# A two-layer hybrid decoder on one core: TensorE's instruction order pinned in the mixing stage

## The chip, the cores and the metric

The kernel runs on one core of a Trainium2 chip. The core has TensorE for matmuls, VectorE (DVE in the rows), ScalarE (ACT) and GpSimd (POOL) for element-wise work, and DMA queues; the kernel's transfers are issued on SyncE's queue (SP). Each engine works through its own list of instructions in order and waits for semaphores that other engines or transfers raise. The metric is device time in microseconds; lower is better.

## The reference, cut to what matters

Two layers work on a sequence of 512 tokens of width 1024 in float32. Each layer is a SwiGLU feed-forward block, a mixing block and a second feed-forward block, each followed by a layer norm:

```python
for l in range(DEPTH):                                   # DEPTH = 2
    x = _layernorm(ALPHA * x + 0.5 * _swiglu(x, ffn1_w_in[l], ffn1_w_out[l]), ...)
    x = _layernorm(ALPHA * x + _hybrid_mixer(x, l, ...), ...)
    x = _layernorm(ALPHA * x + 0.5 * _swiglu(x, ffn2_w_in[l], ffn2_w_out[l]), ...)
```

The mixer makes one wide projection `h = x @ w_in`. Three causal mixers read parts of it: RWKV-7 (8 heads of 64), differential attention (4 heads) and a chunked gated DeltaNet (4 heads of 128). Each result goes through a branch matrix, is weighted by a sigmoid gate made from `h`, and the sum goes through `w_out`:

```python
branches = jnp.einsum('blnc,ncd->blnd', ys, w_branch)
gates = jax.nn.sigmoid(h[..., o3:].reshape(B, L, N_BRANCH, D_MODEL))
merged = jnp.einsum('blnd,blnd->bld', gates, branches)
return merged @ w_out
```

## The kernel before

All matrices are float32 and are multiplied as three products of rounded parts: each weight tile is split into `wh` (a cast on ScalarE) and `wl` (a subtraction on VectorE), and so is the transposed stream (`xTh`, `xTl`). One column of 128 outputs of a projection is thus 8 x 3 = 24 matmuls of 128x512 into one PSUM tile (`proj`, L440). The tiles are `pj` for the mixers, `pz` for DeltaNet's output gate, `pgt` for the merge's gates, `pg` and `pu` in the feed-forward stage.

The mixing stage (`mix`, L1378) is written by Python generators. `main` (L1327) first writes the two lora columns, then twelve units in the order R D R D R R D G G D G G, where R is a pair of RWKV heads, D a head of differential attention and G a DeltaNet head. A unit (`unit`, L1337) writes three projection columns (R and D) or four (G: three `pj`, one `pz`), 24 matmuls each, and then puts a head generator on the list `active`. The first unit is followed by 16 matmuls named `pab`. The first three columns of a stage (both lora columns and one of the first unit) are written ahead of it, under the name `pe`. After the units come three rounds of `merge` (L1290).

A head generator (`rw_pair`, `da_head`, `gdn_head`) yields between its steps. A step holds small matmuls and transposes on TensorE and element-wise work on the other engines. A planner, the class `Estimate`, keeps a clock for each engine from a formula for each instruction; when a step is written it notes in `stage` when the step's results should be there. Every projection yields after six matmuls, and `interleave` (L1372) then writes steps of active heads whose time has come, up to CAP = 1300 ns of TensorE's planned clock. A unit starts only when fewer than WIDTH = 4 heads are active:

```python
while sum(it[0] < 3 for it in self.active) >= WIDTH:
    self.pump(True)
```

Here `pump(True)` writes the next step of a head whose time has come or, when there is none, of the head that is due first. A head leaves the list with its last step. In all three kinds of head that step, or the end of it, is a group of four transposes named `pyT`, of the tile `Y` (R), `dO` (D) or `gO` (G).

In `rw_pair` the transposes `paT` (L933) give `R` on VectorE, and `pW` (L938) reads it in the same step. The step of `pb` splits `sq` first. `inverse` (L680) solves the triangular systems: rows on VectorE, a trip through DRAM, the transposes `iZ` on VectorE, and then matmuls named `ip`.

What is written this way isn't yet the order on an engine. The framework's scheduler walks a timing model of its own and lets an engine take a later instruction when an earlier one is not ready in that model. Only `load_x`, at the kernel's start, pins the order so far. A matmul of the mixing stage passes through `Queue.order` (L73), which adds the edge to the preceding instruction only where `inorder` is set.

Of the kernel before, what the change touches and what calls it, by code (L numbers as in the profile page):

```python
# [134 lines left out]
class Net:  # L135
# [1241 lines left out]

    def mix(self, l):  # L1378
        self.active, self.ys, self.yps, merged = [], [{}, {}, {}], {}, []
        self.interleave(self.main(merged))  # L1380
        acc = [[None, None] for _ in range(NT)]
        self.out_acc(merged[0:4], 0.5 / ALPHA, acc)
        self.out_last(merged[4:8], 0.5 / ALPHA, acc, self.a["ln2_g"][l], self.a["ln2_b"][l])
# [41 lines left out]
```

## Time and profile before

| | before |
|---|---|
| median of 3 runs | 2865.65 us (2860.83 to 2866.03) |
| the profiled execution, its time | 2866.84 us |
| its span, first to last instruction | 2865.0 us |
| mean granted TensorE clock | 0.995 of 2.4 GHz |
| mixing stage, first layer | 395.7 to 1018.7 us |
| mixing stage, second layer | 1817.4 to 2447.2 us |

The page's shares are averages over stages; the rows below go by stage and by instruction. All instructions carry the line L66, which is the helper that records them, so they are told apart by their tiles (`out<-in`). Where a row of the timeline ends in brackets, the engine was idle for so many us before it, until the named engine had written the named tile. Matmul durations are modelled and overlap: the distance from one start to the next tells more than the duration.

### The profile page before, as it was taken

The page shows a single profiled execution, that of the slowest core. Times are in us where ns is not written, and L with a number is a line of the kernel's source. Part 1 is how long each engine was busy: PE and PEld are TensorE (multiplying, and loading weights), DVE is VectorE, ACT ScalarE, POOL GpSimd, SP SyncE. Part 2 cuts the span into 40 slices and gives each one's busy share as a digit, 9 for nine tenths or more (in the row PEclk, how much of TensorE's full clock was granted, in tenths as well). Part 3 has the DMA queues.
Part 4 walks back from the last instruction along what each step waited for, and adds up shares of the span by engine and source line. Part 5 has one row for each costly group of instructions (what it writes and reads, how often), then busy time and mean ns, then how long its engine had stood idle before and what let it go on. Part 6 is the DMA issues. An engine that isn't in the chain of part 4 may idle for free. (4 is left out here: it accounts for less than half of the span.)

```text
span 2865.0 us, 40194 instructions
## 1 busy us (share of the span) xinstructions
PE 2817.8 (98%) x15728; PEld 2333.7 (81%) x15728; DVE 1657.9 (58%) x3760; ACT 1015.4 (35%) x1805; POOL 157.2 (5%) x205
## 2 busy tenths in 40 slices
PE   9999999999999999999999999999999999999998
PEld 8888887778878888888888888777788788888887
DVE  4333568788874463443643335677888745633345
ACT  3222345444543332222422223454445433322222
POOL 1000021010000010000100000210100000100001
PEclk9999999999999999999999999999999999999999
DMA  6433423222223353333533334222222234533332
GB/s 179 126 98 99 141 75 84 67 72 55 71 72 88 101 180 101 98 96 97 155 96 113 101 96 134 82 71 69 69 61 65 72 89 117 163 109 97 96 96 89
DMA packets 436350, 282.18 MB, mean 98 GB/s; under 512 B 39432, under 2 KB 391872, under 8 KB 436160
## 3 DMA queue, kind: packets, MB, share of 16 engines
q1 hardware_dynamic: 436160, 279.60, 33.5%
q8 instruction: 124, 2.03, 0.3%
q14 instruction: 66, 0.54, 0.1%
HBM read 258.31 MB, written 21.25 MB: 98 GB/s over the span
## 5 line engine op out<-in xcount | busy, mean ns | idle before, releaser
L66 DVE TENSOR_TENSOR wl<-wr,wh 128x1024 fp32r<-128x1024 f32 x406 | 500.1, 1232 | 655.7 <-ACT wh L66 652.4
L66 ACT CAST wh<-wr 128x1024 fp32r<-128x1024 f32 x406 | 427.4, 1053 | 1252.4 <-issue 550.9
L66 PE MATMUL pu<-xTh,wh 128*128 128x512 f32 x672 | 261.6, 389 | 0.0
L66 PE MATMUL pu<-xTh,wl 128*128 128x512 f32 x672 | 261.4, 389 | 0.0
L66 PE MATMUL pu<-xTl,wh 128*128 128x512 f32 x672 | 261.4, 389 | 0.0
L66 PE MATMUL oa<-wh,hl 128*128 128x512 f32 x640 | 249.0, 389 | 0.0
L66 PE MATMUL pg<-xTh,wh 128*128 128x512 f32 x640 | 249.0, 389 | 0.0
L66 PE MATMUL pg<-xTl,wh 128*128 128x512 f32 x640 | 249.0, 389 | 0.0
L66 PE MATMUL pg<-xTh,wl 128*128 128x512 f32 x640 | 249.0, 389 | 0.0
L66 PE MATMUL oa<-wh,hh 128*128 128x512 f32 x640 | 249.0, 389 | 0.0
L66 PE MATMUL oa<-wl,hh 128*128 128x512 f32 x640 | 249.0, 389 | 0.0
L66 PE MATMUL pj<-xTh,wh 128*128 128x512 f32 x560 | 229.1, 409 | 0.0
L66 PE MATMUL pj<-xTh,wl 128*128 128x512 f32 x560 | 227.7, 407 | 0.0
L66 PE MATMUL pj<-xTl,wh 128*128 128x512 f32 x560 | 225.7, 403 | 0.0
L66 DVE TENSOR_TENSOR ft<-ft,pu 128x512 f32<-128x512 f32 x84 | 57.7, 687 | 226.5 <-PE pu L66 226.4
L66 PE MATMUL pgt<-xTh,wh 128*128 128x512 f32 x384 | 153.0, 398 | 0.0
L66 PE MATMUL pgt<-xTh,wl 128*128 128x512 f32 x384 | 150.4, 392 | 0.0
L66 PE MATMUL pgt<-xTl,wh 128*128 128x512 f32 x384 | 150.3, 391 | 0.0
L66 PEld LDWEIGHTS pu<-xTh,wl 128*128 128x128 f32 x672 | 126.2, 188 | 26.2
L66 PEld LDWEIGHTS pu<-xTl,wh 128*128 128x128 f32 x672 | 126.2, 188 | 26.0
L66 PEld LDWEIGHTS pu<-xTh,wh 128*128 128x128 f32 x672 | 126.0, 188 | 26.2
L66 PEld LDWEIGHTS pg<-xTh,wh 128*128 128x128 f32 x640 | 120.2, 188 | 25.2
(397 smaller groups left out, 5295.5 us busy)
## 6 DMA issues: line engine op xcount, KB each, us to landing
wr<-in_ffn_w_in_dram SPq DMA_DIRECT2D x176, 512.0 KB
wr<-in_mix_w_in_dram SPq DMA_DIRECT2D x132, 512.0 KB
wr<-in_ffn_w_out_dram SPq DMA_DIRECT2D x88, 512.0 KB
wr<-in_mix_w_branch_dram SPq DMA_DIRECT2D x24, 512.0 KB
xres<-x SPq DMA_DIRECT2D x40, 256.0 KB
x<-xres SPq DMA_DIRECT2D x40, 256.0 KB
wr<-in_mix_w_out_dram SPq DMA_DIRECT2D x16, 512.0 KB
iX<-Xd SPq DMA_DIRECT2D x24, 256.0 KB
```

Of the source, the lines that this page charges most:

```text
L66: r = f(*args, **kw)
```

## The change

While the mixing stage is being written, TensorE's queue object is marked `inorder`. Each TensorE instruction of the stage then gets an edge to the TensorE instruction written just before it, so the scheduler has to keep them in written order. `last` is cleared first, so the stage's first instruction is tied to nothing. The other engines and the transfers are scheduled as before. No instruction is added or removed.

```diff
     def mix(self, l):
         self.active, self.ys, self.yps, merged = [], [{}, {}, {}], {}, []
+        queues = (self.est.tensor,)
+        for q in queues:
+            q.inorder, q.last = True, None
         self.interleave(self.main(merged))
+        for q in queues:
+            q.inorder = False
         acc = [[None, None] for _ in range(NT)]
```

## Rows read from the trace of the kernel before

**Rows 1.** The page: busy us of each engine (share of the span) xinstructions.
```profile
PE 2817.8 (98%) x15728; PEld 2333.7 (81%) x15728; DVE 1657.9 (58%) x3760; ACT 1015.4 (35%) x1805; POOL 157.2 (5%) x205
```
**Rows 2.** Stretches, the two mixing stages: busy us, TensorE clock, DMA share, GB/s.
```profile
395.70:1018.70 623.00, 608.88 (x4117) 495.82 (x4117) 455.38 (x1383) 281.39 (x608) 40.39 (x53) 1.00 0.29 77
1817.40:2447.20 629.80, 617.18 (x4118) 502.27 (x4117) 456.56 (x1382) 281.07 (x607) 39.20 (x52) 0.98 0.28 76
```
**Rows 3.** The page's costliest groups: busy us, mean ns; idle time and its releaser.
```profile
L66 DVE TENSOR_TENSOR wl<-wr,wh 128x1024 fp32r<-128x1024 f32 x406 | 500.1, 1232 | 655.7 <-ACT wh L66 652.4
...
L66 PE MATMUL pu<-xTh,wh 128*128 128x512 f32 x672 | 261.6, 389 | 0.0
...
L66 PE MATMUL pj<-xTh,wh 128*128 128x512 f32 x560 | 229.1, 409 | 0.0
```
**Rows 4.** Timeline of TensorE, projections alone: first and last of 30.
```profile
399.88 0.39 PE L66 MATMUL pj<-xTh,wh 128*128 128x512 f32 x1
...
406.45 0.39 PE L66 MATMUL pj<-xTh,wl 128*128 128x512 f32 x1
```
**Rows 5.** Timeline of TensorE around one projection matmul between small ones.
```profile
781.82 0.39 PE L66 MATMUL pgw<-iZ,rk 128*128 128x128 f32 x2
781.97 0.48 PE L66 MATMUL pj<-xTh,wl 128*128 128x512 f32 x1
782.28 0.38 PE L66 MATMUL pv<-rv,iZ 128*128 128x128 f32 x2
```
**Rows 6.** Stretches from a mixing stage's start: TensorE's matmuls into `pj` alone.
```profile
395.00:556.17 161.17, 97.04 (x379) 1.00 0.27 72
395.00:612.01 217.01, 130.64 (x506) 1.00 0.27 71
395.00:665.95 270.95, 153.54 (x585) 1.00 0.26 69
395.00:717.25 322.25, 187.51 (x715) 1.00 0.27 69
395.00:770.70 375.70, 214.32 (x815) 1.00 0.26 69
...
1817.00:2200.14 383.14, 219.46 (x815) 0.97 0.26 67
```
**Rows 7.** The same stretches, TensorE's matmuls into `pz` alone.
```profile
395.00:665.95 270.95, 5.60 (x24) 1.00 0.26 69
395.00:717.25 322.25, 12.06 (x48) 1.00 0.27 69
395.00:770.70 375.70, 17.94 (x72) 1.00 0.26 69
```
**Rows 8.** Timeline of all engines, the end of one R head.
```profile
716.41 0.69 DVE L66 TENSOR_TENSOR Y<-Y,gn 128x512 f32<-128x512 f32 x1
...
717.25 0.52 PE L66 MATMUL pyT<-ident,Y 128*128 128x128 f32 x3
```
**Rows 9.** Timeline of TensorE from `paT` to `pW` of one R unit.
```profile
498.42 0.60 PE L66 MATMUL paT<-ident,AR 128*128 128x128 f32 x4
498.78 0.48 PE L66 MATMUL pj<-xTh,wh 128*128 128x512 f32 x1
...
499.56 0.40 PE L66 MATMUL pj<-xTh,wh 128*128 128x512 f32 x1
500.83 0.43 PE L66 MATMUL pW<-iZ,R 128*64 128x128 f32 x3 [0.88 <-DVE R L66]
```
**Rows 10.** Timeline of TensorE: one head's `pyT` in the first and second layer.
```profile
556.17 0.52 PE L66 MATMUL pyT<-ident,Y 128*128 128x128 f32 x3 [1.94 <-DVE Y L66]
...
1982.45 0.52 PE L66 MATMUL pyT<-ident,Y 128*128 128x128 f32 x2 [2.52 <-DVE Y L66]
```
**Rows 11.** Stretches after that idle time in the second layer, columns as in Rows 2.
```profile
1982.00:1984.00 2.00, 1.55 (x6) 1.44 (x7) 1.87 (x9) 0.57 (x1) 0.00 (x0) 0.65 0.00 0
1984.00:1986.00 2.00, 2.00 (x9) 1.75 (x8) 0.70 (x2) 0.65 (x2) 0.00 (x0) 0.50 0.00 0
```

## The prediction

> **What bounds the kernel now.** I began with the page's line of engine shares: TensorE is busy for 98% of the span [rows 1], so this time goes down only if TensorE issues less or waits less, and it goes up by every wait that nothing fills. The reader should see there how little is left to win. Next came the stretches of the two mixing stages, the only ones that the change touches: 623.0 and 629.8 us, with TensorE busy for 608.9 and 617.2 of them [rows 2]. So 14.1 and 12.6 us are plainly idle. VectorE is busy for 455 us in either stage (73%), which makes it the engine that TensorE's small matmuls wait for. Last I read TensorE's own timeline, to see in which order its instructions run today, and compared that with the order in which the code writes them.
>
> The plain stream of projections runs at (406.45 - 399.88) / 29 = 0.2266 us from one matmul to the next [rows 4]. I use this step, and not the modelled durations of 389 and 409 ns [rows 3], as the price of one wide matmul. The heads' small matmuls are sprinkled into that stream.
>
> **What the change does to the order.** It adds no instruction and no byte. It ties each TensorE instruction of the stage to the one written before it. Today the scheduler lets a later instruction go first when, by its reckoning, the one in front has no data yet; the fillers are the wide projection matmuls. Afterwards TensorE stands still in those places.
>
> The largest of them can be counted. Before it writes the columns of a unit, `unit` drives the active heads until fewer than WIDTH = 4 are left. Each head's last TensorE step is its `pyT` group. So in the written order a `pyT` must come before the first projection of that unit. The units' columns are known (2 lora, 3 per R or D unit, 4 per G unit, 24 wide matmuls each, the first three columns done early). By the order in which heads start and in which their `pyT` groups run today, four heads are active at five unit starts: the fourth R unit and each of the four G units. At the third R, third D and fourth D units one of the four has already ended, so nothing is forced there.
>
> The fourth R unit may start after 14 columns, 336 wide matmuls. By the `pyT` at 556.17 us there have run 379 [rows 6]: 43 too early. The first G unit: 20 columns, 480; by 612.01 us 506 have run: 26. The second G unit: 24 columns, 576; by 665.95 us 585 `pj` and 24 `pz` have run [rows 6, 7]: 33. The third G unit: 31 columns, 744; by 717.25 us 715 + 48: 19. The fourth: 35 columns, 840; by 770.70 us 815 + 72: 47. Together 168 wide matmuls of each layer now run ahead of a step that is written before them; the second layer's last count is the same 815 [rows 6]. Priced at 0.2266 us they are 38.1 us per layer that today cover a wait.
>
> **How much of this cover turns into waiting.** Nothing, if data lies ready and TensorE only comes late to it; all of it, if the data comes no earlier. The nearest rows say mostly the second: at the third G unit, VectorE's last write of `Y` ends at 716.41 + 0.69 = 717.10 us, and `pyT` starts at 717.25, 0.15 us later [rows 8]. There TensorE is waiting for VectorE whatever it does meanwhile. And at 556.17 `pyT` idled 1.94 us even behind its five fillers [rows 10]. Against this: a filler overshoots the moment of readiness by half a matmul on average, and seven columns (168 / 24) fewer in these stretches means seven fewer weight splits of 1.23 us [rows 3] on VectorE in the middle of the chains that are waited for. I take two thirds: 25.4 us per layer, between bounds of one half (19) and all (38).
>
> **The small shifts elsewhere.** Some steps read, on TensorE, what VectorE or ScalarE makes within the same step: `pW` after `R`, `pb` after the split of `sq`, `ip` after the transposes of `iZ`. The row to look at: `paT` at 498.42, four projections, then `pW` at 500.83, idle 0.88 us for `R` [rows 9]. In written order these four come afterwards, so the wait grows by 4 x 0.2266 = 0.9 us. Per layer there are 4 R units with two such places and 8 inversions: 16 x 0.9 = 14.5 us, of which a good third lies inside the forced stretches already counted. I take 9 (estimate), bounds 3 and 16, since heads wait at the same time and one wait serves several.
>
> **What is won.** After a small group the next wide matmul takes 782.28 - 781.97 = 0.31 us instead of 0.2266 [rows 5], 0.08 us more. Some 38 such returns per layer vanish when the fillers leave the forced stretches (estimate, the 168 in gaps of four or five): 3 us.
>
> **The clock.** After the 2.52 us idle before `pyT` in the second layer [rows 10] the granted clock reads 0.65 and then 0.50, the lower level of 1.2 GHz, for the next two stretches of 2 us [rows 11]: (0.35 + 0.50) x 2 = 1.7 us lost. The first layer had 1.94 us idle at the same place [rows 10] and kept 1.00 throughout [rows 2]. The change makes some five waits of this length in each layer (one at the end of each forced stretch, estimate); if every second one is followed by such a spell, with the spell's loss partly inside other waits, that is 4 us per layer.
>
> The Trainium skill (TensorE: Matmul & The Clock Gate, section "HAM oscillation — how this bites in real kernels") says that a matmul kernel which waits between bursts drops to the low clock at each wait and pays for the warm-up again. By that rule all ten new waits would pay, 17 us in place of 8; the second layer's row agrees with it, the first layer's does not.
>
> **The sum.** Per layer 25.4 + 9 + 4 - 3 = 35.4 us, 70.8 for both. The profiled execution took 2866.84 us (span 2865.0 and 1.84 around it): 2937.6. It lies 1.2 us above the median of the three runs, so I say 2936 us. What is queued behind a waiting matmul are the next unit's projections, and behind these ScalarE's `sh` and `cv` passes and the weight casts; they only slide, as TensorE is the engine that all of them follow. Weight loads on SP's queue slide with them; DMA engines are busy for 0.29 [rows 2], so nothing collides. The merges after the last unit hold no small work at their end that could win anything back.
>
> **Rivals.** (1) *It pays, by fewer switches.* Mixing projections show up to 409 ns against 389 in the feed-forward stage [rows 3]: 20 ns x 1680 `pj` is 34 us at most that the sprinkling costs, and 26.7 us are idle [rows 2]. If a fixed order halved both and the forced waits were filled, about 30 us would go: 2836. It decides where fewer than 15 / 0.2266 = 66 of the 168 fillers of a layer become waits. The late `Y` speaks against it; the idle rows, which show that the scheduler's guess is often wrong, for it. Chance 0.08.
> (2) *Only the single shifts cost.* While a chain is late, other heads' small work that today runs behind `pyT` may be written ahead of it and fill the gap. Then 9 + 2 - 3 = 8 us per layer: 2881. Against it: the scheduler would have run such work in place of a projection, had it been ready. Chance 0.13.
> (3) *It costs more.* One late small matmul also holds back small ones of other heads, which today slip past as well, and all waits come with the low clock: 38 + 16 + 9 = 63 us per layer, 2992 and beyond. The trace shows such slipping only in passing. Chance 0.12.
> (4) *The order was nearly there*, no difference: the counts speak against it. Chance 0.04.
>
> **How the numbers follow.** The forecast has 0.63. Its own bounds are 19 + 3 - 4 = 18 and 38 + 16 + 8 = 62 us per layer, 2901 to 2990. The range from 2876 to 2995 takes in rival 2 and the lower edge of rival 3. A difference under 0.2% can't be told from none here. Faster 0.08, within 0.2% 0.05, slower 0.87.
>
> **What would show it.** In the profile after, each of the five counts should read exactly 336, 480, 576, 744 and 840 before its `pyT`, with idle rows "<-DVE Y", "<-DVE iZ", "<-DVE dsc" on TensorE; TensorE's idle time should grow by 60 us or more over the two stages, and the feed-forward stages stay as they are. Returns from small to wide should be fewer. The prediction is wrong if the counts are met and yet TensorE idles no more than today (the data was ready), or if the stage's clock falls well under 0.95 (the spells weigh more than I take).

## The result and the profile after

The pinned kernel takes 3019.41 us (median of 4 runs, 3012.95 to 3020.03) against 2865.84 us (4 runs, 2860.83 to 2870.67): ratio 1.0531, 95% interval 1.0508 to 1.0554. It is slower, as forecast, but by 154 us where I had 71, and above the range. The profiled execution took 3020.03 us, its span is 3018.3 us and its mean granted clock 0.973.

The page's line of engine shares, to be read against [rows 1]:

```profile
PE 2860.4 (95%) x15728; PEld 2376.4 (79%) x15728; DVE 1666.7 (55%) x3760; ACT 1018.6 (34%) x1805; POOL 153.6 (5%) x205
```

The same instructions ran. TensorE's busy time grew by 43 us and its share still fell from 98% to 95%. The stretches of the two mixing stages, columns as in [rows 2]:

```profile
396.04:1098.19 702.15, 633.89 (x4116) 520.04 (x4114) 460.43 (x1383) 282.75 (x607) 38.15 (x53) 0.95 0.26 69
1896.94:2599.91 702.97, 634.65 (x4116) 520.62 (x4115) 460.13 (x1382) 282.64 (x606) 37.85 (x52) 0.95 0.25 68
```

Against [rows 2] they grew by 79.2 and 73.2 us, 152 of the 153 us by which the span grew: the feed-forward stages did not move. TensorE is plainly idle for 68.3 us in each (702.15 - 633.89 and 702.97 - 634.65), where it was idle for 14.1 and 12.6: 54.1 + 55.7 = 109.8 us more. The clock reads 0.95 where it read 1.00 and 0.98. VectorE's busy time is within 6 us of before.

The counts of projections before the five `pyT` groups that close a head before a unit may start, columns as in [rows 6], with the busy times of the other engines that touch the tile behind TensorE's; first those into `pj`:

```profile
395.00:578.75 183.75, 88.41 (x336) 64.69 (x336) 11.44 (x16) 13.61 (x22) 0.91 0.23 60
395.00:638.49 243.49, 126.07 (x480) 90.48 (x480) 16.43 (x23) 19.14 (x31) 0.92 0.24 61
395.00:704.32 309.32, 144.31 (x552) 103.48 (x552) 23.11 (x32) 21.75 (x35) 0.92 0.23 59
395.00:768.40 373.40, 182.37 (x696) 130.69 (x696) 32.54 (x45) 27.88 (x45) 0.93 0.23 60
395.00:829.37 434.37, 200.93 (x768) 144.17 (x768) 39.17 (x54) 29.91 (x48) 0.93 0.23 58
```

and those into `pz`, as in [rows 7]:

```profile
395.00:704.32 309.32, 7.61 (x24) 5.16 (x24) 0.69 (x1) 0.58 (x1) 0.92 0.23 59
395.00:768.40 373.40, 13.61 (x48) 9.52 (x48) 1.37 (x2) 1.17 (x2) 0.93 0.23 60
395.00:829.37 434.37, 19.49 (x72) 13.95 (x72) 2.05 (x3) 1.74 (x3) 0.93 0.23 58
```

336, 480, 552 + 24 = 576, 696 + 48 = 744, 768 + 72 = 840: the five forecast numbers to the last matmul. From the end of the last projection to the `pyT` that ends each forced stretch TensorE then did this (length, TensorE's busy time, clock, DMA share, GB/s):

```profile
541.84:578.75 36.91, 27.87 (x361) 0.86 0.13 32
637.32:638.49 1.17, 1.17 (x34) 1.00 0.00 0
683.54:704.32 20.78, 17.77 (x312) 1.00 0.11 28
763.78:768.40 4.62, 1.29 (x9) 1.00 0.23 55
804.05:829.37 25.32, 17.68 (x139) 0.82 0.13 33
```

The idle time in them is 9.0 + 0 + 3.0 + 3.3 + 7.6 = 23.0 us (23.3 in the second layer). I had forecast 25.4. The other 68.3 - 23.0 = 45.3 us of the stage's idle time stand at other places, where I had added 9. Here are the longest of the profile's waits of TensorE over the whole program, those in the forced stretches included (total us, times, longest):

```profile
PE pG L66 <- DVE gg L66: 14.7, 2, 7.4
PE pk L66 <- DVE gL L66: 14.1, 16, 1.9
PE pyT L66 <- DVE gO L66: 12.2, 6, 2.8
PE pb L66 <- ACT sqh L66: 11.9, 4, 3.3
PE pW L66 <- DVE R L66: 11.2, 8, 3.1
PE ppT L66 <- DVE dsc L66: 11.1, 8, 3.5
PE pkk L66 <- ACT AR L66: 9.6, 8, 1.4
```

The longest of all, `pG`, lies far from any forced stretch, in the DeltaNet scalars near the stage's start. Here is TensorE's timeline around it, after:

```profile
421.24 0.39 PE L66 MATMUL pj<-xTh,wl 128*128 128x512 f32 x1
428.98 0.61 PE L66 MATMUL pG<-gg,m_le 128*128 128x16 f32 x2 [7.36 <-DVE gg L66]
```

and before:

```profile
427.55 0.39 PE L66 MATMUL pj<-xTl,wh 128*128 128x512 f32 x1
429.91 0.40 PE L66 MATMUL pG<-gg,m_le 128*128 128x16 f32 x2 [1.97 <-DVE gg L66]
```

The data for `pG` came at about the same moment in both. What differs is how many projections had run by then. The stretch up to `pG`, `pj` alone, before:

```profile
395.00:429.91 34.91, 26.36 (x113) 21.15 (x113) 3.55 (x5) 4.62 (x8) 1.00 0.24 64
```

and after:

```profile
395.00:428.98 33.98, 18.50 (x78) 14.50 (x78) 2.87 (x4) 2.53 (x4) 0.93 0.23 62
```

113 against 78: the scheduler had let 35 projections slip past `pG`, almost six whole groups of six, at a place for which I had allowed nothing.

### The profile page after: what moved, and what is told of

Its sections match the earlier page's. It is cut to its first block, busy times and chain, and to the rows that moved or that the text cites. A ratio compares the mean times of both kernels' runs of the same rounds, so it can differ in the third digit from the quotient of the medians.

```text
span 3018.3 us, 40200 instructions
## 1 busy us (share of the span) xinstructions
PE 2860.4 (95%) x15728; PEld 2376.4 (79%) x15728; DVE 1666.7 (55%) x3760; ACT 1018.6 (34%) x1805; POOL 153.6 (5%) x205
## 5 line engine op out<-in xcount | busy, mean ns | idle before, releaser
L66 PE MATMUL pj<-xTh,wh 128*128 128x512 f32 x560 | 239.9, 428 | 0.0
```

Source lines behind the costliest of these rows:

```text
L66: r = f(*args, **kw)
```

## The experiments

Three theories stood at the start. A: a late small matmul costs only because no wide one fills the wait, and this goes on all over the stage. B: it costs because other heads' small matmuls stand behind it too. C: the forced stretches are the main cause. In all the kernels the instructions are written in the same order as in the change, unless said otherwise; what differs is which edges tie them. The flag `wide` is set around the matmuls of `proj`, `gdn_ab` and `merge`, the flag `forced` around the loop with `pump(True)` in `unit`; `tie(ins, to)` adds the edge that `order` added.

**Two chains.** Wide ones keep their order among themselves, small ones theirs; a wide one may pass a small one.

```diff
-        if self.inorder and self.last is not None:
-            self.est.tc.add_manual_dep(ins, self.last.name, ...)
+        if self.inorder:
+            k = self.est.wide
+            if self.tail[k] is not None:
+                self.tie(ins, self.tail[k])
+            self.tail[k] = ins
```

> TensorE's wide matmuls (projections, gates, branches) are tied to each other in written order and the heads' small ones to each other, but wide ones may pass small ones. Theory A, only the lost filling by wide matmuls costs: 2866 us, within 0.5%. Theory B, a late small matmul holds back the small ones of other heads: at least 2920 us, since here this holding back is still in force. Theory C, the forced stretches at unit starts are the main cost: also about 2866, since they are filled again.

Measured: 2853.66 us, ratio 0.9967 (0.9955 to 0.9979). The whole loss is gone though every small matmul still waits for every earlier small one. So B falls: where wide ones fill the waits, the order of the small ones costs nothing. A and C had the same forecast here, and it was met.

**Free within a run.** Small ones between two wide ones may change places; nothing passes a wide one.

```diff
+            if self.est.wide:
+                for i in self.small or [self.tail]:
+                    if i is not None:
+                        self.tie(ins, i)
+                self.small, self.tail = [], ins
+            else:
+                if self.tail is not None:
+                    self.tie(ins, self.tail)
+                self.small.append(ins)
```

> The complement: between two wide matmuls the small ones may change their order, but nothing passes a wide one. Theory A: 3005 to 3019 us, little is won. Theory B: below 2980 us. Theory C: about as A.

Measured: 3014.31 us, ratio 1.0526 (1.0502 to 1.0550), the same as the change. B falls a second time, from the other side.

**Only the forced stretches tied.** Wide matmuls, and the small ones written in the forced stretches, keep their order; all other small ones are free.

```diff
+        if self.inorder and not (self.est.forced or self.est.wide):
+            return
```

> Only wide matmuls and the small ones written in the forced stretches are tied; small ones elsewhere are free as before. Theory A: a third of the loss, 2917 us. Theory C: 2965 us or more.

Measured: 2915.79 us, ratio 1.0189 (1.0158 to 1.0219), that is 45 to 63 us. By my terms for these stretches, the clock and the returns, 2 x (25.4 + 4 - 3) = 53 us. A's 2917 us is met, and C falls: these stretches alone make about a third of the loss.

**The forced stretches untied, all else tied.** The mirror image.

```diff
+        if self.inorder and self.est.forced:
+            return
```

> The pinned order, but TensorE instructions written while a unit start drives heads to their end are not tied, so the next unit's projections may pass them. Theory A, with 18 of the 54 us of added idle time per layer in these stretches: a third of 153 us comes back, 2968 us. Theory C (the prediction's ratio of 25 to 9): two thirds or more come back, 2915 us or less. Theory B: between, as the held small ones of these stretches are free too, about 2940.

Measured: 3008.30 us, ratio 1.0508 (1.0483 to 1.0533): only 11 us come back by the medians (7 by the ratios, whose intervals overlap) of the 54 that the stretches cost alone. The numbers of all three theories missed. The trace shows why at one place. A long wait in the first forced stretch, in the change's timeline of TensorE:

```profile
561.85 0.47 PE L66 MATMUL ppT<-ident,dsc 128*128 128x128 f32 x1 [3.54 <-DVE dsc L66]
```

the count of `pj` before it:

```profile
395.00:561.85 166.85, 88.41 (x336) 64.69 (x336) 11.44 (x16) 13.61 (x22) 0.92 0.24 62
```

the same wait in the kernel with the stretches untied:

```profile
560.69 1.04 PE L66 MATMUL ppT<-ident,dsc 128*128 128x128 f32 x4 [3.54 <-DVE dsc L66]
```

and the count before that one:

```profile
395.00:560.69 165.69, 90.23 (x342) 65.78 (x342) 11.45 (x16) 13.61 (x22) 0.93 0.24 63
```

The wait has the same 3.54 us, only six projections later, 342 instead of 336. The wide ones now run on until the next small matmul that is tied in, which was written one group of six later, and there the head is as late as before. Six matmuls are 1.4 us by [rows 4]; if all five stretches in both layers behave like this one, which was not read, they make 14 us at most. The shares of a loss in a fixed order therefore don't add up: taking one group of edges out leaves its lateness to the next group.

**How much slack is wanted.** A wide matmul need only follow the small ones that were written at least SLIP wide ones before it.

```diff
+            if self.est.wide:
+                self.seen.append(self.small)
+                for i in (self.tail, self.seen[max(0, len(self.seen) - 1 - SLIP)]):
+                    if i is not None:
+                        self.tie(ins, i)
+                self.tail = ins
+            else:
+                for i in (self.tail, self.small):
+                    if i is not None:
+                        self.tie(ins, i)
+                self.small = ins
```

The two expectations use the letter C for a different rival: that a late small matmul wants far more room than six.

> The change with slack: a wide matmul need only follow the small ones that were written at least six wide ones before it, so up to six wide ones (1.4 us at 0.2266 us) may pass a late small one; wide ones keep their order, small ones theirs. Theory A (only the lost filling costs): of the 68 us that TensorE is idle between instructions in each mixing stage of the changed kernel, the many waits under 1.4 us go and each longer one loses 1.4 us, which by the waits over 0.9 us leaves some 25 to 40 us per stage; with part of the low clock gone: 2900 to 2945 us. Theory C (what a late small matmul needs is far more than six wide ones, in the forced stretches above all): over 2960 us.

> As the run with a slack of six, but with twenty-four wide matmuls (5.4 us). Theory A: no wait outside the first one for the pG tile (7.4 us) is longer than 5.4 us, and the five forced stretches together wait 23 us per stage, 4.6 us each, so nearly all of the loss is back: 2860 to 2885 us. Theory C: the stretches, in which the kernel before ran 19 to 47 wide ones, still lack half of theirs: 2890 to 2920 us.

Measured: 2955.21 us with six (ratio 1.0326, 1.0299 to 1.0353), 2887.89 us with twenty-four (1.0084, 1.0061 to 1.0107). Both fall between the two forecasts, the first 10 us above A's range and 5 under C's, the second 3 above A's and 2 under C's. By the medians 64 us come back with the first six, 67 with the next eighteen, and 34 more with no limit (two chains). So the lateness has a long tail: over half of the loss is still there when six wide ones may pass.

**Matmuls that do nothing, ahead of the waits.** The change, with 126 extra wide matmuls per stage, at ten places (the expectation counts eleven), whose tile is overwritten by the real group behind them; they add work and take no wait away.

```diff
+    def fill(self, net, p, n):
+        for _ in range(n):
+            self.order(self.eng.matmul(p, net.r_id, net.neg, start=True, stop=True, ...).ins)
...
+        pf = self.psum(name="pG")
+        self.nc.tensor.fill(self, pf, 30)
```

> The changed kernel with its order, and 126 wide matmuls per mixing stage that compute nothing (their tile is overwritten behind them) written ahead of eleven of its longest waits: 30 before the pG matmuls, 7 to 14 before two pb, two pyT of R, one pW, one ppT, one pyT of D and two of G; sized a little shorter than the waits that they stand in (28.6 of 68 us per stage). They take no wait away. If the low clock comes from TensorE standing idle there (some 17 us per stage over the clock of the kernel before), the time falls by 10 to 30 us, to 2990 to 3010 us, and the mean granted clock rises from 0.973 towards 0.985. If the low clock has another cause, the time stays within 5 us of 3019 or rises.

Measured: 2990.86 us, ratio 1.0446 (1.0425 to 1.0467), clock 0.991: with 2 x 28.6 us of matmuls added the kernel is 28.6 us faster by the medians (24 by the ratios) than the change without them. Stretches of the change around the wait for `pG`, columns as in [rows 2]:

```profile
427.00:429.00 2.00, 0.02 (x1) 0.02 (x1) 1.66 (x11) 0.00 (x0) 0.00 (x0) 0.50 0.76 216
429.00:431.00 2.00, 2.00 (x8) 1.90 (x9) 0.31 (x2) 0.21 (x1) 0.00 (x0) 0.50 0.06 9
```

and with the filling:

```profile
429.00:431.00 2.00, 2.00 (x11) 1.68 (x11) 0.00 (x0) 0.35 (x2) 0.00 (x0) 1.00 0.03 1
```

After the idle 7.36 us TensorE runs at 0.50, the level of 1.2 GHz, and issues 8 instructions in 2 us; after 6.97 us of empty work it runs at 1.00 and issues 11. The page of the filled kernel:

```profile
PE 2883.4 (97%) x15980; PEld 2395.0 (80%) x15980; DVE 1667.3 (56%) x3760; ACT 1017.8 (34%) x1805; POOL 153.8 (5%) x205
```

The 252 empty matmuls are 57.1 us by the step of [rows 4], so by that estimate the others took 2826 us where they took 2860.4 in the change, 34 us less. Idle time fell by less than was put in, from 157.9 to 2987.6 - 2883.4 = 104.2 us. So at least 24 to 29 of the 154 us are the clock's at these ten places.

**Other durations in the planner.** VectorE at least 0.21 us, ScalarE dearer.

```diff
-        self.vector = q(nc.vector, lambda op, n, k: 70 + n * (0.52 if op in (...) else 1.04))
+        self.vector = q(nc.vector, lambda op, n, k: max(210, 130 + 1.05 * n))
...
-        return 80 + n / 1.2 + (94 if ... else 0)
+        return 130 + n / 1.1 + (94 if ... else 0) + (200 if k.get("accum_out") is not None else 0)
```

> The changed kernel, with other durations in the planner that decides when a step's instructions are written: VectorE at least 0.21 us (before: 0.07 us and 1.04 ns per element), ScalarE 0.05 us more and 0.2 us for an accumulated output. If the small matmuls are late because the planner takes VectorE and ScalarE for faster than they are, they are written later, more wide ones stand before each, and the time falls by a third of the loss or more: 2960 us or less. If the lateness comes from steps that write an instruction of VectorE and the matmul that needs it side by side, whatever the planner thinks, the time stays within 1% of the change: 2990 to 3045 us.

Measured: 3013.59 us, ratio 1.0527 (1.0503 to 1.0551): no difference from the change that can be told, as the second theory forecast. By the page TensorE is idle for 3010.9 - 2841.4 = 169.5 us against 3018.3 - 2860.4 = 157.9: the waits changed places, and there is no less of them.

**The same, with steps cut in two.** A `yield` where a step wrote an element-wise operation and right behind it the matmul that needs it.

```diff
+        yield
         p = self.psum((128, 4, 128), "pkk")
...
+        parts = self.split(sq, "sq")
+        yield
         pb = self.psum(name="pb")
...
+        yield
         p = self.psum((128, 4, 128), "pW")
...
             nc.vector.transpose(out=Z[e], in_=X[e])
+        yield
...
                 for j in range(2):
                     self.mm(pk[:, j, q, :], KQ[0][:, s], KQ[j][:, s], start=True, stop=True)
+            for q in range(2):
+                tt = 2 * tp + q
                 STT(...)
```

> The run with the other planner durations, and five places at which a step that wrote an instruction of VectorE, ScalarE or GpSimd and right behind it the matmul that needs it is cut in two, so that the planner can write other work between them (ahead of pkk, of pb behind its split, of pW, of the inverse's first product, and the gated heads' pk matmuls of both q before the two operations on VectorE). If the ordinary waits come from such steps, the waits for these five (pk 7.1, pkk 3.8, pb 2.0, pW 1.6, the inverse's iZ 8.9 us in one stage of the run without the cuts) mostly go, some 15 to 20 us per stage with the clock that comes back: 2970 to 2985 us, against 3014 us without the cuts. If the lateness only moves to the next small matmul in the chain, under 10 us: 3004 us or more.

Measured: 2982.48 us, ratio 1.0414 (1.0390 to 1.0437), 31 us less than without the cuts. TensorE's waits without the cuts:

```profile
PE ip L66 <- DVE iZ L66: 37.6, 13, 6.8
PE pk L66 <- DVE gL L66: 17.4, 16, 1.9
PE pW L66 <- DVE R L66: 13.6, 6, 5.2
PE pkk L66 <- ACT AR L66: 9.9, 8, 1.4
...
PE pyT L66 <- DVE gO L66: 9.5, 2, 4.8
```

and the largest with them:

```profile
PE pyT L66 <- DVE Y L66: 16.8, 4, 6.4
PE pyT L66 <- DVE gO L66: 16.7, 6, 4.2
PE pyT L66 <- DVE dO L66: 11.5, 4, 3.4
PE pU L66 <- DVE M L66: 10.2, 4, 4.7
```

The first four lines, 78.5 us, are all but gone (2.0 us are left, of `iZ`), and the time falls by 31: much of the rest stands at the heads' ends (`pyT`) and at `pU` instead. The steps that depend on themselves are a true cause of waits, worth about a fifth of the loss here (the cuts also let other steps be written in between, and this was not separated), and once more a removed wait uncovers the next.

**One chain at a time.** Two chains had come out below the kernel before; which of them does it? This is the chain of the small ones; for the wide ones the condition is `self.est.wide`.

```diff
-        if self.inorder and self.last is not None:
-            self.est.tc.add_manual_dep(ins, self.last.name, ...)
-        self.last = ins
+        if self.inorder and not self.est.wide:
+            if self.last is not None:
+                self.tie(ins, self.last)
+            self.last = ins
```

> One of the two chains of the version that was 0.33% faster than the kernel before: the small matmuls of the stage keep their written order among themselves, the wide ones are free. If the gain comes from the small ones' order, about 2854 us (ratio 0.9955 to 0.998); if it comes from the wide ones' order, about 2864 us (0.999 to 1.001).

> The other chain: the wide matmuls keep their written order among themselves, the small ones are free. If the gain of the version with both chains comes from the wide ones' order, about 2854 us (ratio 0.9955 to 0.998); if from the small ones', about 2864 us (0.999 to 1.001). That a wide matmul held back by its chain costs something would show as over 1.001.

Measured: small ones tied 2856.25 us, ratio 0.9969 (0.9958 to 0.9979); wide ones tied 2864.59 us, ratio 0.9997 (0.9986 to 1.0008). The gain of 0.3% over the kernel before is the small ones' order. The two mixing stages of the kernel with the small ones tied:

```profile
395.80:1016.80 621.00, 610.29 (x4116) 495.62 (x4115) 453.29 (x1383) 281.98 (x608) 40.88 (x53) 0.99 0.29 78
1815.40:2437.30 621.90, 610.26 (x4116) 495.63 (x4115) 453.50 (x1382) 281.75 (x606) 40.65 (x52) 0.99 0.29 77
```

and the one wait of a `pyT` for `Y` that its timeline still has:

```profile
1974.99 0.63 PE L66 MATMUL pyT<-ident,Y 128*128 128x128 f32 x4 [0.48 <-DVE Y L66]
```

The second stage is 7.9 us shorter than in [rows 2]. The wait of 2.52 us in it [rows 10] is 0.48 now, and the clock in the four us behind, 0.65 and 0.50 in [rows 11], reads 1.00. But that wait is a small part: of the 7.9 us, 6.9 are TensorE's busy time (617.18 against 610.26) and 1.0 is idle time, and the mean clock differs between executions of one kernel. At the same mean clock the small chain is still ahead: 2857.9 us (mean of 5) against 2862.3 (mean of 6) at 0.996, and 2855.2 (6) against 2859.7 (3) at 0.997. So about half of the 9 us by the medians goes with the clock. What makes the other half was not shown.

**Two chains, planner and cuts together.**

> The two chains (wide ones may pass small ones) with the other planner durations and the cuts. If steps written nearer to when they can run leave less to fill, it is a little faster than the two chains alone (2854 us): 2840 to 2852 us. If the scheduler fills every wait anyway, 2850 to 2860 us, no difference that can be told.

Measured: 2862.28 us, ratio 0.9992 (0.9980 to 1.0003), 2 us above the second range. Nothing is gained, and what the small chain gained is lost: where wide ones may pass, other durations and finer steps do not help. The fastest kernels of this study are the two chains and the small chain, which can't be told apart.

## Why the prediction was right or wrong

**Right: what bounds, where, and which sign.** The loss lies in the two mixing stages, in idle time of TensorE and in its clock, with the feed-forward stages unmoved. The five counts came out exactly. Returns from a small matmul to a wide one, counted in the traces, fell from 172 to 131 in each stage, 41 where I had 38; what they gave back can't be read apart from the clock. One sign did not come: the waits of `ip` for `iZ` shrank from 4.2 to 1.1 us.

**Right: the forced stretches.** Forecast 25.4 us per layer, read 23.0 after (1.94 us stood at the first of them before [rows 10]), and tied alone they cost 45 to 63 us where my terms gave 53. Singly the forecast was rougher: the stretch before the first G unit, with 26 matmuls to lose, had no wait at all, since its data lay ready, and the first one waited 9.0 us where two thirds of 43 x 0.2266 were 6.5. That the sum is so near is in part luck.

**Wrong: the step "the small shifts elsewhere".** This is the term that failed: 9 us per layer, bounds 3 and 16. Idle time outside the forced stretches is 45.3 us after; the whole stage had 14.1 before [rows 2], so it grew by at least 31. I took one row, `paT`, four projections, `pW` [rows 9], for the size of all such shifts, and only three kinds of step for their places. Added up by tile over both layers, the waits of the three that I had named, `pb`, `pW` and `ip`, went from 12.1 us in the stages before to 39.4 outside the forced stretches after: 13.7 per layer, above my 9 and inside its bounds. Those of `pG`, `pk` and `pkk`, which I had named nowhere, went from 5.1 to 33.7: another 14.3 per layer that stood at nothing in my sum. The timeline of the row that I had taken, `paT` to `pW` in the first R unit, after, and of the same pair in the third R unit:

```profile
521.05 0.60 PE L66 MATMUL paT<-ident,AR 128*128 128x128 f32 x4
522.43 0.77 PE L66 MATMUL pW<-iZ,R 128*64 128x128 f32 x10 [0.78 <-DVE R L66]
...
639.67 0.60 PE L66 MATMUL paT<-ident,AR 128*128 128x128 f32 x4
643.41 0.48 PE L66 MATMUL pW<-iZ,R 128*64 128x128 f32 x2 [3.14 <-DVE R L66]
```

The row that I had picked did not grow (0.88 before, 0.78 after), though the four projections that I had priced did go: 282 had run before the first pair's `pW` where there were 286. Its sister, which had not waited before, became 3.14 us. In the kernel before, seven projections ran in that pair, 506 by 612.01 us [rows 6] and 513 by its `pW` at 615.29:

```profile
395.00:615.29 220.29, 132.60 (x513) 92.80 (x513) 16.43 (x23) 19.71 (x32) 1.00 0.27 70
```

Seven are 1.6 us by the step, half of the wait. The other half is VectorE's. Its last write of `R`, in the kernel before:

```profile
614.38 0.68 DVE L66 TENSOR_TENSOR R<-paT,nn 128x512 f32<-128x512 f32 x1
```

and after:

```profile
640.01 1.21 DVE L66 TENSOR_TENSOR wl<-wr,wh 128x1024 fp32r<-128x1024 f32 x1
...
642.59 0.68 DVE L66 TENSOR_TENSOR R<-paT,nn 128x512 f32<-128x512 f32 x1
```

It began 1.24 us after `paT` (613.14) in the kernel before and 2.92 us after it (639.67) now, with a weight split of 1.21 us begun in between. VectorE's order, which nothing pins, had moved with TensorE's.

The longest wait, `pG`, was on no list of mine, because I looked only for steps that wait for themselves. The counting that I had done for the five `pyT`, written against run, had to be done for every small group: it gives 35 for `pG`. Slack of six wide ones returns 64 of the 154 us, so a lag of up to one group, which is all that I had allowed outside the forced stretches, was less than half of it.

**Wrong in size: the clock.** Forecast 4 us per layer, by one spell after every second of five waits. The filling shows at least 12 to 14. There are more long waits than the five, and of seven of them in the first layer after, those of 2.42, 2.76, 2.81, 3.14, 3.54 and 7.36 us were followed by 0.50 and only the one of 1.92 us by 1.00. Their length alone does not sort them: at the one of 2.42 us the clock already read 0.50 while TensorE waited (500 to 502 us), and a wait of 1.88 us, for `pk` at 716.97, is followed by 0.50 too. The Trainium skill's rule that I weighed (TensorE: Matmul & The Clock Gate, "HAM oscillation — how this bites in real kernels": a kernel that waits for transfers between its bursts starts cold after each wait) would have had 17 us for the ten waits. It was nearer than my half, and six of these seven rows agree with it, though here the waits are for VectorE.

**The sum.** The two stages grew by 152.3 us, and the rows split it without a rest: TensorE is idle for 109.8 us more and, with the same instructions, busy for 42.5 us more (25.0 and 17.5). In my terms that is 25.4 and 9 per layer for the first and 4 less 3 for the second. By the estimate beside the filling, 34 of the 42.5 us are the clock's at the waits filled there. What the other 8 are was not settled; the clock still reads 0.991 with the filling, against 0.995 before, so part may be low clock at the waits left unfilled.

**The rivals.** Rival 3 named a time, 2992 and beyond, that the result meets, but its first mechanism is refuted twice: small matmuls held back behind a late one cost nothing measurable. Its second, that the waits come with the low clock, was the better guess: it had 9 us per layer for that, and 12 to 14 were measured. Rivals 1, 2 and 4 fall by the time. What rival 1 hoped for exists in small: a fixed order of the small ones alone gains 0.3%, though not by fewer switches: the returns from small to wide are 172 per stage there as in the kernel before.

## What to carry to other kernels

Before an order is pinned, count for every group that waits how many independent instructions run ahead of it today against how many are written ahead of it, and do so for all such groups and not only at the places that look forced. The lags say where waits can come, not what they will cost: 26 of them gave no wait where the data lay ready, and elsewhere VectorE's order moved too. Tie the instructions that have a real order among them and leave those free that fill the gaps: with the same small order the kernel was 5% slower with the wide ones tied in, and 0.3% faster with them loose. In a chain of late steps, price an edit by a run and not by the waits that it removes: 78.5 us of them gave 31 us.

## What the runs showed that I had not expected

Work that computes nothing can pay: 252 wide matmuls, 57 us of TensorE's time by the step of [rows 4], written into waits that stay, raised the mean clock from 0.973 to 0.991 and took 24 to 29 us off the time.
